# A gated S5 and attention layer: chunk outputs with C loaded once, transfers spread over three queues, and TensorE's order written out

## The chip, the core and the metric

The kernel runs on one core of a Trainium2 chip. The metric is the device time of one execution in microseconds (us). TensorE multiplies (its results go to PSUM, in banks of 128 x 512 float32), VectorE and ScalarE evict PSUM and do the elementwise work, GpSimd does elementwise work in SBUF only, and SyncE (SP) issues transfers. ScalarE and GpSimd can issue transfers as well; each engine runs its instructions, the issues among them, strictly in the order in which they stand in its program.

## The reference, cut to what matters

One layer on x (512 tokens, 1024 channels), all in float32:

```python
h = rms_norm(x, norm_w)
u_s, z_s, q, k, v, z_a, r_s, r_a = split(h @ w_in)      # 1024 -> 9216 columns
# S5 branch: 64 groups of 16 channels, 64 complex states each
#   state[t] = Abar * state[t-1] + Bbar @ u[t];   y = Re(C @ state) + D * u
g = gelu(y);  y_s = (g * sigmoid(g @ w_glu) * silu(z_s)) @ w_ssm_out
# three groups of dilated sliding-window attention, merged by their softmax sums
y_a = (attention(q, k, v) * silu(z_a)) @ w_attn_out
out = x + (sigmoid(r_s) * y_s + sigmoid(r_a) * y_a) @ w_o
```

## The kernel before, in words

**Matmuls.** Every weight matmul is done as three in a rounded format, with operands split into a high and a low part: `mm3` (lines 107 to 110). `load_w` (162) fetches a weight tile (SP issues it, line 166), ScalarE makes the high part (line 93), VectorE the low part (line 95). There are two raw slots and three split slots. A channel-major unit, `cm_unit` (172), is 8 x 3 matmuls of 128x512, accumulated in one of three PSUM banks named `pj`. In what follows such a unit with its eviction is a *filler*: za (4 of them), zs (8), rs (8), ra (8) for the gates, v0 for the values of group 0. The token-major unit v (`v_granule`, 572) has 96 matmuls of half the width. The list `order` (127 to 128) says in which order they are taken, and `plan` lists the weight loads in the same order. rs and ra end in a tanh on ScalarE (lines 469, 477) and a store to DRAM; zs ends in a product on VectorE and a store. `n_ra` ra units are in `order`, the others stand in the last attention round (lines 1018 to 1023), between scores and values and after the values.

**The S5 branch.** The sequence is cut into 64 blocks of 8 tokens, and the groups of channels into 8 *chunks* of 8 groups.
- `u_unit` (256) brings u of a chunk to DRAM, `load_u` (238) reloads it with positions on the partitions.
- *State stage*: `w_unit` (263) makes the chunk's input coefficients (VectorE, GpSimd and VectorE again: `coef`, 244 to 254) and transposes them into W; `x_unit` (275) makes from W and u the input of the scan.
- *Scan*: some 75 VectorE steps over all groups (`scan_work`, 636 to 640), traced in ten portions with a filler ahead of each.
- *Chunk outputs* (lines 755 to 787): `ca_unit` (667) loads C of the chunk, swaps its halves on GpSimd, transposes both and forms the output coefficients in one of three buffers `ab` (line 418); `m_unit` (692) forms a table M: eight small matmuls, four copies on ScalarE, the D term added on GpSimd (703), a store to DRAM (704) and a reload in another arrangement (707). `s_unit` (712) copies the states (eight copies on ScalarE), `y_unit` (724) multiplies U by M and the states by the coefficients, `g_unit` (738) transposes the result back and applies GELU into `gT_hi` and `gT_lo`. The loop over j traces m(j+2), a filler, y(j), ca(j+3), the reload of U(j+2), s(j+1), g(j-1).
- After it stands the GLU matmul (958 to 970).

**What sets the order.** The kernel is written with a framework that puts each engine's instructions in order itself: a planner simulates the program and takes, for each engine, the ready instruction that was traced first. The order of the trace is thus a priority, and where an instruction isn't ready by the planner's clock, a later one goes ahead of it. The order is fixed when the program is built. Small PSUM results share four banks (`bank`, 85). Tiles named by a `tag` share memory: a new tile waits until the last user of the old one is done.

Of the kernel before, what the change touches and what calls it, by code (L numbers as in the profile page):

```python
# [20 lines left out]
P = 128  # L21
# [4 lines left out]
G = 64  # L26
# [26 lines left out]
def tile_hybrid_block(ctx: ExitStack, tc: tile.TileContext, x, positions, norm_w, w_in, lam_re, lam_im,  # L53
                      log_dt, b_re, b_im, c_re, c_im, d_skip, w_glu, q_norm_w, k_norm_w, w_ssm_out,
                      w_attn_out, w_o, out, dbg=None):
    nc = tc.nc
    pe, act, dve, pool, sp = nc.tensor, nc.scalar, nc.vector, nc.gpsimd, nc.sync
    dbg = dbg or {}
# [53 lines left out]
    plan, loaded, look = [], [], 2  # L112
    n_ra = 2
    lo_w = [dve]
# [141 lines left out]
    def u_unit(j, ps=None):  # L256
        if ps is None:
            ps = cm_unit(hT_hi, hT_lo)
        uT = t2k("uT")
        act.copy(uT.rearrange("p (h r c) -> p r c h", h=2, r=4), ps.rearrange("p (r c h) -> p r c h", r=4, h=2))  # L260
        sp.dma_start(ud[j].rearrange("q g s c -> g q (s c)"), uT)

    def w_unit(j):
        ba = ab[j % 2][:, 0:8 * T * Q].rearrange("p (g k q) -> p g k q", g=8, k=T)
        g8 = slice(8 * j, 8 * j + 8)
        coef(ba, j, BB[:, g8], BB2[:, g8], 1, T + 1, ab[2], pool)
        W = big.tile([P, 8, P], F32, name="W", tag=("s6a", "s6b")[j % 2])
# [138 lines left out]


    dd = big.tile([P, 4, G, Q], F32, name="dd", tag="s1")
    D1, D2, BB, BB2 = (dd[:, i] for i in range(4))
# [21 lines left out]
    pool.memset(sgn[64:128], -1.0)  # L431

    Ws = {}

# [25 lines left out]
    def zs_unit(c):  # L460
        ps = cm_unit(hT_hi, hT_lo)
        z = t2k("z")
        silu2(z, ps)
        sp.dma_start(gd[0, c], z)

    def rs_unit(c):
        ps = cm_unit(hT_hi, hT_lo)
        th = t2k("th")
        act.activation(th, ps, AF.Tanh, scale=0.5)
        sp.dma_start(gd[1, c], th)  # L470
# [193 lines left out]
    pool.memset(zer, 0.0)  # L664
    sp.dma_start(kd[:, :, :, 128:240].rearrange("j q g k -> (j q) g k"), zer)

    def ca_unit(j):

        cn = sml.tile([P, 2, P], F32, name="cn")
        rows = slice(j * P, (j + 1) * P)  # L670
        sp.dma_start(cn[:, 0, 0:64], c_re[0].rearrange("g p n -> (g p) n")[rows])
        sp.dma_start(cn[:, 0, 64:128], c_im[0].rearrange("g p n -> (g p) n")[rows])
        pool.tensor_copy(cn[:, 1, 0:64], cn[:, 0, 64:128])
        pool.tensor_copy(cn[:, 1, 64:128], cn[:, 0, 0:64])
        ps = bank("cps")
        for i in range(2):
            pe.transpose(ps[:, i * P:(i + 1) * P], cn[:, i], ident)
        p12 = sml.tile([P, 2, 8, Q], F32, name="p12")
        p12f = p12.rearrange("p a g q -> p a (g q)")
        dve.tensor_scalar(p12f[:, 0], ps[:, 0:P], sgn, None, op0=ALU.mult)  # L680
        act.activation(p12f[:, 1], ps[:, P:2 * P], AF.Copy, scale=-1.0)
        ca = ab[j % 3].rearrange("p (g k q) -> p g k q", g=8, k=9)
        for h in range(2):
            coef(ca[:, 4 * h:4 * h + 4], 2 * j + h, p12[:, 0, 4 * h:4 * h + 4], p12[:, 1, 4 * h:4 * h + 4], 0, 9,
                 abt[:, 3 * nca:], dve)

        dg = sml.tile([Q, 8, Q], F32, name="dg")
        sp.dma_start(dg.rearrange("q g p -> q (g p)"), d_skip[0:1, rows].to_broadcast([Q, P]))
        pool.tensor_tensor(dg, dg, ident[0:Q, 0:Q].unsqueeze(1).broadcast_to([Q, 8, Q]), op=ALU.mult)
        return ca, dg  # L690

    def m_unit(j, ca, dg):

        kt = big.tile([Q, 8, T, Q], F32, name="kt", tag=("s7a", "s7b")[j % 2])
        ps = bank("kps")
        for gg in range(8):
            a, b = gg % 4, gg // 4
            pe.matmul(ps[32 * a:32 * a + Q, b * P:(b + 1) * P], BB[:, 8 * j + gg, :], ca[:, gg, 1:9, :],
                      start=True, stop=True, skip_group_check=True, tile_position=(0, 32 * a))
        kv = kt.rearrange("q (b a) k p -> q a b (k p)", a=4)  # L700
        for a in range(4):
            act.copy(kv[:, a], ps[32 * a:32 * a + Q, 0:2 * P].rearrange("q (b m) -> q b m", b=2))
# [4 lines left out]
        sp.dma_start(M.rearrange("p (g k) -> p g k", g=8),  # L707
                     bass.AP(tensor=kj.tensor, offset=kj.offset, ap=[[Q, T], [8 * 240, Q], [240, 8], [1, P]]))
        M = M.rearrange("p (g k) -> p g k", g=8)
        return M  # L710
# [43 lines left out]

    cas, dgs, Ms, Us, Ss_, ysbs = {}, {}, {}, {}, {}, {}
    for j in range(3):
        cas[j], dgs[j] = ca_unit(j)
        if j < 2:
            Ms[j] = m_unit(j, cas[j], dgs[j])
    n_scan = 10  # L760
    for i in range(n_scan):
        filler()
        for f in scan_work[i * len(scan_work) // n_scan:(i + 1) * len(scan_work) // n_scan]:
            f()

    uss = big.tile([P, 4, 512], F32, name="uss", tag="s6b")
    for j in range(2):
        Us[j] = load_u(j, uss[:, j % 2])
    Ss_[0] = s_unit(0)
    for j in range(8):  # L770
        if j + 2 < 8:
# [9 lines left out]
        if j > 0:  # L781
            g_unit(j - 1, ysbs.pop(j - 1))
    if fill:
        filler()
# [310 lines left out]
```

## Time and profile before

| | |
|---|---|
| median of 3 runs | 743.52 us (743.5 to 743.62) |
| profiled execution | 745.33 us, its span 743.5 us |
| mean granted TensorE clock | 0.983 |
| TensorE, VectorE, ScalarE, GpSimd busy | 94%, 63%, 45%, 23% of the span |
| moved by DMA | 85.51 MB, 115 GB/s in the mean |

A row of the profile names the line of the kernel, the engine, the operation, the output tile and its inputs, and the shapes; `x` and a number is a count. In rows of groups there follow busy time in us, the mean of one in ns, and the idle time of the engine before them with what ended it. In a timeline the first two numbers are start and duration in us. SPq is SP's queue of issues. PE is TensorE, DVE VectorE, ACT ScalarE, POOL GpSimd. A float32 matmul of the small kind stands as two records.

### The profile page before, as it was taken

To read this page: it belongs to the slowest core of one execution; us is meant where nothing else is said; L and a number is where in the kernel's file an instruction comes from. 1 tells how busy PE (TensorE), PEld (TensorE's weight loads), DVE (VectorE), ACT (ScalarE), POOL (GpSimd) and SP (SyncE) were. 2 spreads that over 40 slices of the span, in tenths; PEclk is the share of its full clock that TensorE was granted. 3 is DMA by queue.
4 is the path that set the end of the run, shared out by engine and by line. 5 is a ranking of instruction groups with operands and counts; after the bars stand their busy time and mean duration, and the time that the engine had idled before them with its cause. 6 is when DMAs were issued, how large, how long until landed. Compare 5 with 4: busy or idle time off the path is not lost.

```text
span 743.5 us, 13321 instructions
## 1 busy us (share of the span) xinstructions
PE 702.2 (94%) x5221; PEld 615.8 (83%) x5221; DVE 468.4 (63%) x958; ACT 336.7 (45%) x628; POOL 168.7 (23%) x304
## 2 busy tenths in 40 slices
PE   3699999999979688999999999999999999999998
PEld 2687788788857477888899999899999989778997
DVE  6768757989867454674336679667747654536631
ACT  6443544233388574433143475464446435433310
POOL 3345631110001001550001224142304311200000
PEclk9899999999999899999999999999999999999999
DMA  9754654674637765447324212213211321356321
GB/s 203 129 143 110 159 114 105 144 178 118 120 101 138 136 132 143 154 133 217 91 80 120 86 57 85 59 30 98 85 46 57 95 77 57 109 179 226 124 100 57
DMA packets 156014, 85.51 MB, mean 115 GB/s; under 512 B 40232, under 2 KB 148144, under 8 KB 155824
## 3 DMA queue, kind: packets, MB, share of 16 engines
q1 hardware_dynamic: 155936, 84.66, 44.1%
q8 instruction: 41, 0.67, 0.4%
q14 instruction: 21, 0.17, 0.1%
q10 hardware_dynamic: 16, 0.00, 0.0%
HBM read 73.18 MB, written 11.47 MB: 114 GB/s over the span
## 4 chain that ended last, share of the span: by engine, by line
PE 78%; DMA 8%; DVE 6%; SPq 3%; ACT 2%; issue 2%; POOL 0%; DVEq 0%; ACTq 0%
PE pj L110 21%; PE pj L109 21%; PE pj L108 21%; DMA w_raw<-in_w_in_dram 4%; PE ot L926 3%; PE ptp L940 2%; PE sps L870 2%; PE qtp L827 1%; DMA kd<-kt 1%; DVE w_lo L95 1%; PE xps L282 1%; DMA dd<-kd 1%; PE wps L271 1%; DMA gd<-th 1%; DVE scn L610 1%
## 5 line engine op out<-in xcount | busy, mean ns | idle before, releaser
L93 ACT ACTIVATE w_hi<-w_raw 128x1024 fp32r<-128x1024 f32 x100 | 105.9, 1060 | 200.6 <-PE pj L109 89.4
L95 DVE TENSOR_TENSOR w_lo<-w_raw,w_hi 128x1024 fp32r<-128x1024 f32 x98 | 124.2, 1268 | 64.1 <-ACT w_hi L93 62.9
L108 PE MATMUL pj<-hT_hi,w_hi 128*128 128x512 f32 (+1 forms) x344 | 135.0, 395 | 9.7 <-ACT w_hi L93 5.6
L109 PE MATMUL pj<-w_lo,hT_hi 128*128 128x256 f32 x512 | 144.0, 281 | 0.0
L110 PE MATMUL pj<-w_hi,hT_lo 128*128 128x256 f32 x512 | 143.9, 281 | 0.0
L108 PE MATMUL pj<-w_hi,hT_hi 128*128 128x256 f32 x512 | 143.8, 281 | 0.0
L109 PE MATMUL pj<-hT_lo,w_hi 128*128 128x512 f32 (+1 forms) x344 | 133.5, 389 | 0.4 <-DVE hT_lo L228 0.4
L110 PE MATMUL pj<-hT_hi,w_lo 128*128 128x512 f32 (+1 forms) x344 | 133.3, 388 | 0.1
L109 PEld LDWEIGHTS pj<-w_lo,hT_hi 128*128 128x128 f32 x512 | 96.2, 188 | 1.4 <-issue 0.7
L108 PEld LDWEIGHTS pj<-w_hi,hT_hi 128*128 128x128 f32 x512 | 96.0, 188 | 1.1 <-issue 0.9
L110 PEld LDWEIGHTS pj<-w_hi,hT_lo 128*128 128x128 f32 x512 | 96.0, 188 | 0.7
L108 PEld LDWEIGHTS pj<-hT_hi,w_hi 128*128 128x128 f32 x344 | 67.0, 196 | 23.1 <-ACT w_hi L93 5.8
L110 PEld LDWEIGHTS pj<-hT_hi,w_lo 128*128 128x128 f32 x344 | 66.5, 193 | 14.5 <-issue 0.8
L109 PEld LDWEIGHTS pj<-hT_lo,w_hi 128*128 128x128 f32 x344 | 66.8, 194 | 13.5 <-DVE hT_lo L228 0.8
L814 POOL TENSOR_TENSOR rt<-qraw,tC 128x256 f32<-128x256 f32 x12 | 16.5, 1371 | 127.0 <-DVE qraw L807 93.0
L109 PE MATMUL pj<-w_lo,mT_hi 128*128 128x256 f32 x128 | 36.2, 283 | 0.0
L110 PE MATMUL pj<-w_hi,mT_lo 128*128 128x256 f32 x128 | 36.2, 283 | 0.0
L108 PE MATMUL pj<-w_hi,mT_hi 128*128 128x256 f32 x128 | 36.2, 283 | 0.0
L849 ACT ACTIVATE Pt<-Pt,st 128x256 f32<-128x256 f32 (+1 forms) x64 | 31.0, 487 | 5.0 <-DVE st L847 4.8
L799 DVE TENSOR_REDUCE ssq<-qsq 128x8 f32<-128x512 f32 x24 | 16.4, 685 | 26.3 <-ACT qsq L798 26.2
L835 ACT ACTIVATE qkp<-qtp,wcol 128x512 fp32r<-128x512 f32 (+1 forms) x32 | 20.7, 685 | 20.7 <-PE qtp L827 15.6
L796 ACT COPY qraw<-pj 128x512 f32<-128x512 f32 x24 | 14.1, 586 | 35.0 <-PE pj L110 34.8
(272 smaller groups left out, 1368.5 us busy)
## 6 DMA issues: line engine op xcount, KB each, us to landing
w_raw<-in_w_in_dram SPq DMA_DIRECT2D x40, 512.0 KB
w_raw<-in_w_in_dram SPq DMA_DIRECT2D x64, 256.0 KB
dd<-kd SPq DMA_DIRECT2D x8, 512.0 KB
w_raw<-in_w_glu_dram SPq DMA_DIRECT2D x8, 512.0 KB
w_raw<-in_w_ssm_out_dram SPq DMA_DIRECT2D x8, 512.0 KB
w_raw<-in_w_o_dram SPq DMA_DIRECT2D x8, 512.0 KB
x_all<-in_x_dram SPq DMA_DIRECT2D x4, 512.0 KB
ud<-uT SPq DMA_DIRECT2D x8, 256.0 KB
```

What stands on the lines that cost most here:

```text
L93: act.activation(hi, src, AF.Copy, scale=scale)
L95: e.tensor_tensor(lo, src, hi.bitcast(F32), op=ALU.subtract)
L108: pe.matmul(o, lh, rh, start=first, stop=False, skip_group_check=True)
L109: pe.matmul(o, lh, rl, start=False, stop=False, skip_group_check=True)
L110: pe.matmul(o, ll, rh, start=False, stop=last, skip_group_check=True)
L799: dve.tensor_reduce(sq[:, 2 * b:2 * b + 2], s.rearrange("p (r h d) -> p r h d", r=2, h=4), AX.X, ALU.add)
L814: pool.tensor_tensor(t1, rh[:, :, :, 0:16], cv.broadcast_to([P, NB * 2, 2, 16]), op=ALU.mult)
L835: act.activation(hi, ps[sl], AF.Copy, scale=w)
L849: act.activation(o, o, AF.Exp, bias=nm, scale=-1.0, accum_out=st[:, kind, 1, h, b:b + 1])
L870: pe.matmul(pss[h][:, cols], QT[x_][po, 0, cb], KA[y_][po, ks], start=n == 0, stop=n == 2, skip_group_check=True)
L926: pe.matmul(o, v, pts[h][:, (2 * i + k) * P:(2 * i + k + 1) * P], start=first, stop=kind == 1 and b == NB - 1 and k == 1, skip_group_check ...
L940: pe.transpose(ps[:, (2 * i + k) * P:(2 * i + k + 1) * P], Pt[:, h, kind, 2 * bb + i, k * P:(k + 1) * P], ident)
```

## The change: what it does

- C is loaded as a whole into one tile by two transfers on ScalarE's queue; the swapped transposes are taken by two matmuls with an identity. Before, each chunk had two loads on SP's queue and two copies on GpSimd. D is loaded once and transposed; each chunk then multiplies the identity with its column.
- `ca_unit` is cut in two: `p_unit` (transposes and their two scalings, both on ScalarE now) and `ca_unit` (the coefficients). The coefficients have four buffers instead of three, and the product's temporary has a tile of its own. ca(3) is traced ahead of the loop, ca(j+4) in it.
- Queues: the reloads of u, the zs stores, the stores and reloads of the kernel tables go to GpSimd's; the stores of u, rs and ra go to ScalarE's. The weights stay on SP's.
- TensorE's order: with `issue_after`, each block of the loop is put behind the last TensorE instruction traced before it. The filler goes first in each chunk, and a filler stands ahead of the loop.
- The order of fillers: rs ahead of v0 and v, and four ra units in `order` instead of two.
- The table kt has one buffer instead of two; W's two buffers are one tile.

```diff
+    class pe:
+        @staticmethod
+        def matmul(*a, **k):
+            last[0] = nc.tensor.matmul(*a, **k)
...
+    def queued():
+
+        return tc.issue_after(last[0].ins)
...
-    n_ra = 2
+    n_ra = 4
...
-    order = [("za", c) for c in range(NP)] + [("zs", c) for c in range(KT)] + [("v0", 0), ("v", 0)]
-    order += [("rs", c) for c in range(KT)] + [("ra", c) for c in range(n_ra)]
+    order = [("za", c) for c in range(NP)] + [("zs", c) for c in range(KT)] + [("rs", c) for c in range(KT)]
+    order += [("v0", 0), ("v", 0)] + [("ra", c) for c in range(n_ra)]
...
-        sp.dma_start(Uj, ud[j].rearrange("q g s c -> s q g c"))
+        pool.dma_start(Uj, ud[j].rearrange("q g s c -> s q g c"))
...
-        sp.dma_start(ud[j].rearrange("q g s c -> g q (s c)"), uT)
+        act.dma_start(ud[j].rearrange("q g s c -> g q (s c)"), uT)
...
+    cna = big.tile([P, 8, P], F32, name="cn", tag="s6a")
+    act.dma_start(cna[:, :, 0:64], c_re[0].rearrange("(j g) p n -> (g p) j n", j=8))
+    act.dma_start(cna[:, :, 64:128], c_im[0].rearrange("(j g) p n -> (g p) j n", j=8))
...
-    abt = big.tile([P, 4096], F32, name="ab", tag="s5")
-    ab = [abt[:, i * nca:(i + 1) * nca] for i in range(3)]
+    abt = big.tile([P, 4 * nca], F32, name="ab", tag="s5")
+    ab = [abt[:, i * nca:(i + 1) * nca] for i in range(4)]
...
-        sp.dma_start(gd[0, c], z)
+        pool.dma_start(gd[0, c], z)
...
-        sp.dma_start(gd[1, c], th)
+        act.dma_start(gd[1, c], th)
...
-        sp.dma_start(rad[c], th)
+        act.dma_start(rad[c], th)
...
+    def p_unit(j):
+
         ps = bank("cps")
-        for i in range(2):
-            pe.transpose(ps[:, i * P:(i + 1) * P], cn[:, i], ident)
+        pe.transpose(ps[:, 0:P], cna[:, j], ident)
+        for h in range(2):
+            pe.matmul(ps[64 * h:64 * h + 64, P:2 * P], cna[:, j, 64 - 64 * h:128 - 64 * h], ident, start=True, stop=True,
+                      skip_group_check=True)
         p12 = sml.tile([P, 2, 8, Q], F32, name="p12")
         p12f = p12.rearrange("p a g q -> p a (g q)")
-        dve.tensor_scalar(p12f[:, 0], ps[:, 0:P], sgn, None, op0=ALU.mult)
+        act.activation(p12f[:, 0], ps[:, 0:P], AF.Copy, scale=sgn)
         act.activation(p12f[:, 1], ps[:, P:2 * P], AF.Copy, scale=-1.0)
...
-        sp.dma_start(kd[j, :, :, 0:128], kt.rearrange("q g k p -> q g (k p)"))
+        pool.dma_start(kd[j, :, :, 0:128], kt.rearrange("q g k p -> q g (k p)"))
...
-        sp.dma_start(M.rearrange("p (g k) -> p g k", g=8),
+        pool.dma_start(M.rearrange("p (g k) -> p g k", g=8),
...
     n_scan = 10
     for i in range(n_scan):
         filler()
         for f in scan_work[i * len(scan_work) // n_scan:(i + 1) * len(scan_work) // n_scan]:
             f()
-
+        if i == 1:
+            p_unit(3)
     uss = big.tile([P, 4, 512], F32, name="uss", tag="s6b")
     for j in range(2):
         Us[j] = load_u(j, uss[:, j % 2])
     Ss_[0] = s_unit(0)
+    cas[3] = ca_unit(3)
+    filler()
     for j in range(8):
+        with queued():
+            filler()
         if j + 2 < 8:
-            Ms[j + 2] = m_unit(j + 2, cas[j + 2], dgs[j + 2])
-        filler()
-        ysbs[j] = y_unit(j, cas.pop(j), Ms.pop(j), Us.pop(j), Ss_.pop(j))
-        if j + 3 < 8:
-            cas[j + 3], dgs[j + 3] = ca_unit(j + 3)
+            with queued():
+                Ms[j + 2] = m_unit(j + 2, cas[j + 2])
+        with queued():
+            ysbs[j] = y_unit(j, cas.pop(j), Ms.pop(j), Us.pop(j), Ss_.pop(j))
+        if j + 4 < 8:
+            with queued():
+                p_unit(j + 4)
+            cas[j + 4] = ca_unit(j + 4)
...
-            g_unit(j - 1, ysbs.pop(j - 1))
-    if fill:
+            with queued():
+                g_unit(j - 1, ysbs.pop(j - 1))
+    with queued():
         filler()
```

More of the change, by code (lines that the diff above doesn't have):

```diff
@@ L56, in tile_hybrid_block, with transpose @@
     nc = tc.nc
-    pe, act, dve, pool, sp = nc.tensor, nc.scalar, nc.vector, nc.gpsimd, nc.sync
+    act, dve, pool, sp = nc.scalar, nc.vector, nc.gpsimd, nc.sync
+    last = [None]
+    class pe:
+        @staticmethod
+        def matmul(*a, **k):
+            last[0] = nc.tensor.matmul(*a, **k)
+        @staticmethod
+        def transpose(*a, **k):
+            last[0] = nc.tensor.transpose(*a, **k)
+    def queued():
+        return tc.issue_after(last[0].ins)
     dbg = dbg or {}
@@ L266, in w_unit @@
         coef(ba, j, BB[:, g8], BB2[:, g8], 1, T + 1, ab[2], pool)
-        W = big.tile([P, 8, P], F32, name="W", tag=("s6a", "s6b")[j % 2])
+        W = wt[:, j % 2]
         for h in range(2):
@@ L405, in tile_hybrid_block @@
         pool.tensor_scalar(A4[sl, 0, 1], ATv[sl, 1, h, :, 0], -1.0, None, op0=ALU.mult)
+    d64 = scr([G, Q])
+    act.dma_start(d64, d_skip[0].rearrange("(g q) -> g q", g=G))
+    dcol = cst.tile([Q, G], F32, name="dcol")
+    ps = bank("dps")
+    pe.transpose(ps[0:Q, 0:G], d64, ident[:G, :G])
+    act.copy(dcol, ps[0:Q, 0:G])
+    cna = big.tile([P, 8, P], F32, name="cn", tag="s6a")
+    act.dma_start(cna[:, :, 0:64], c_re[0].rearrange("(j g) p n -> (g p) j n", j=8))
+    act.dma_start(cna[:, :, 64:128], c_im[0].rearrange("(j g) p n -> (g p) j n", j=8))
     dd = big.tile([P, 4, G, Q], F32, name="dd", tag="s1")
@@ L431, in tile_hybrid_block @@
     pool.memset(sgn[64:128], -1.0)
+    wt = big.tile([P, 2, 8, P], F32, name="W", tag="s6b")
     Ws = {}
@@ L664, in tile_hybrid_block @@
     pool.memset(zer, 0.0)
[L665 to L674, printed above, removed]
+    pool.dma_start(kd[:, :, :, 128:240].rearrange("j q g k -> (j q) g k"), zer)
@@ L687, in ca_unit, with m_unit @@
+    def m_unit(j, ca):
         dg = sml.tile([Q, 8, Q], F32, name="dg")
[L688 to L694, printed above, removed]
+        pool.tensor_tensor(dg, ident[0:Q, 0:Q].unsqueeze(1).broadcast_to([Q, 8, Q]),
+                           dcol[:, 8 * j:8 * j + 8].unsqueeze(2).broadcast_to([Q, 8, Q]), op=ALU.mult)
+        kt = big.tile([Q, 8, T, Q], F32, name="kt", tag="s7a")
@@ L753, in g_unit @@
         split(gT_hi[:, j], gT_lo[:, j], q, scale=0.5)
[L755 removed]
+    cas, Ms, Us, Ss_, ysbs = {}, {}, {}, {}, {}
     for j in range(3):
[L757 removed]
+        p_unit(j)
+        cas[j] = ca_unit(j)
         if j < 2:
[L759 removed]
+            Ms[j] = m_unit(j, cas[j])
     n_scan = 10
```

13 lines of the change are left out of this document (9 added, 4 removed).

## Prediction

> **What bounds the kernel now.** I read the page first, then busy time by stretch, then TensorE's waits, its order of instructions, and what the other engines do in the same stretch.
>
> ```profile
> span 743.5 us, 13321 instructions
> PE 702.2 (94%) x5221; PEld 615.8 (83%) x5221; DVE 468.4 (63%) x958; ACT 336.7 (45%) x628; POOL 168.7 (23%) x304
> ```
>
> TensorE is busy 702.2 of 743.5 us, so a gain can only come from the 41 us in which it is idle and from stretches in which it is slow. Busy time by stretch (first the scan, from the last state unit on, then the chunk outputs), once for all work and once for the weight-stream matmuls alone (tile pj):
>
> ```profile
> core 0: us, PE busy (x) PEld busy (x) DVE busy (x) ACT busy (x) POOL busy (x), PEclk, DMA share, GB/s
> 118.00:204.80 86.80, 86.80 (x464) 70.39 (x464) 79.22 (x110) 29.67 (x49) 12.22 (x14) 1.00 0.60 135
> 204.80:292.50 87.70, 71.48 (x798) 56.84 (x797) 49.42 (x71) 62.24 (x139) 7.61 (x19) 0.92 0.61 125
> ```
>
> ```profile
> 118.00:204.80 86.80, 84.00 (x402) 68.40 (x402) 6.12 (x9) 7.00 (x12) 1.00 0.60 135
> 204.80:292.50 87.70, 43.95 (x170) 32.88 (x169) 0.00 (x0) 5.28 (x9) 0.92 0.61 125
> ```
>
> In the scan TensorE never rests and VectorE is busy 79.2 of 86.8 us. In the chunk outputs TensorE is idle 16.2 us and its clock falls to 0.92. Only 170 wide matmuls stand there, 7 fillers of 24 (rs3 to rs7, ra0, ra1): the planner ran TensorE ahead during the scan and used up the rest. What TensorE waits for there, and its order in time:
>
> ```profile
> PE kps L698 <- DVE ab L254: 5.8, 2, 3.4
> PE pj L108 <- ACT th L469: 4.1, 1, 4.1
> PE yps L731 <- issue: 2.6, 1, 2.6
> PE yps L733 <- ACT uss L721: 2.1, 1, 2.1
> PE yps L731 <- DMA dd<-kd: 1.5, 1, 1.5
> ```
>
> ```profile
> 222.67 0.41 PE L698 MATMUL kps<-ab,dd 128*16 128x128 f32 x8
> ...
> 226.15 0.48 PE L108 MATMUL pj<-hT_hi,w_hi 128*128 128x512 f32 x1
> 226.47 0.40 PE L109 MATMUL pj<-hT_lo,w_hi 128*128 128x512 f32 x1
> ...
> 231.60 0.40 PE L110 MATMUL pj<-hT_hi,w_lo 128*128 128x512 f32 x1
> ...
> 245.50 0.79 PE L108 MATMUL pj<-hT_hi,w_hi 128*128 128x512 f32 x1 [4.10 <-ACT th L469]
> 246.09 0.63 PE L109 MATMUL pj<-hT_lo,w_hi 128*128 128x512 f32 x1
> 246.52 0.63 PE L110 MATMUL pj<-hT_hi,w_lo 128*128 128x512 f32 x1
> ```
>
> From 226.47 to 231.60 lie 22 matmuls, 0.233 us each: a filler is 24 of them, 5.6 us. One chunk's own work (m, y, p, g units) takes 222.67 to 226.15, 3.5 us. So 170 x 0.233 + 8 x 3.5 = 67.7 us at most fill 87.7 us: **at least 20 us are lost** in this stage, 16.2 as idle time and the rest because after a wait of 4.1 us the matmuls start 0.43 us apart. These 20 us are what the change can win.
>
> **The change, part by part.** *TensorE's order.* Every block of a chunk now stands behind the block before it, so TensorE cannot run past y(0), which needs the end of the scan. Ahead of y(0) stand za3, zs0-7, rs0-2. Before, v0 and v were done there too: 24 wide matmuls (5.6 us) and 96 of half width. Thirteen fillers are 312 wide ones, 72.8 us, and 84.0 - 72.8 leaves 11.2 us for the 96. TensorE thus reaches y(0) 16.8 us sooner, and after m(2) (0.7 us, from two pieces like the one at 222.67) stands there at 204.8 - 16.8 + 0.7 = 188.7. Queued behind it are p(4) and rs3, and behind those the stores and evictions that read them.
>
> *When y(0) may start.* That is VectorE's scan:
>
> ```profile
> 117.54 0.35 DVE L680 TENSOR_SCALAR p<-cps,sgn 128x128 f32<-128x128 f32 x1 [4.76 <-PE cps L677]
> ...
> 204.89 0.69 DVE L612 TENSOR_TENSOR Xs<-Xs,scn 128x512 f32<-128x512 f32 x1
> ```
>
> ```profile
> L95 DVE TENSOR_TENSOR w_lo<-w_raw,w_hi 128x1024 fp32r<-128x1024 f32 x14 | 17.3, 1239 | 5.7 <-ACT w_hi L93 5.6
> ...
> L253 DVE TENSOR_TENSOR ab<-p,AT 128x576 f32<-128x576 f32 x7 | 5.2, 749 | 0.0
> ```
>
> ```profile
> 207.33 0.34 PE L733 MATMUL yps<-ab,uss 128*64 128x64 f32 x4 [2.10 <-ACT uss L721]
> ```
>
> The scan ends at 204.89 + 0.69 = 205.6 and y(0)'s state half starts 1.75 us later. Three weight splits fewer: -3.7. The 5.7 us that VectorE stands before a split, because the weights land late on SP's crowded queue: -3.5 of them. Three p scalings (0.35) go to ScalarE: -1.0. ca(0) no longer waits for its C transpose, so its six operations of 0.75 fit partly into the 4.76 us of idle time at 117.5: -2.5 of 4.5. ca(3) has a buffer of its own and slips into the scan, five operations more than today: +3.7. Sum -7.0: scan end 198.6, y(0) at 200.3. With every wait won back and ca(3) left behind the scan it is 192, with no wait won back and nothing brought forward 208. I take 200.3, the middle of the two. TensorE idles about 11.6 us before y(0), and starts slow again: 12 matmuls at 0.43 instead of 0.233 is 2.3 us, of which I count 2.0.
>
> *From y(0) to the first GLU matmul.* Left are rs3-7, v0, v (worth two), ra0-3: 12 fillers' worth, 67.2 us, and 8 x 3.5 = 28: 95.2 us. ScalarE must keep up. In the second stretch it is busy 62.24 us over 139 instructions, 0.448 each, and a full chunk has 20 of them (state copies 8, kt 4, g 4, y, th, w_hi, p 1 each): 9.0 us. It gains the second p scaling and the issue of a store:
>
> ```profile
> L681 ACT ACTIVATE p<-cps 128x128 f32<-128x128 f32 x4 | 1.1, 280 | 0.1
> ```
>
> ```profile
> 237.39 1.44 SPq L470 DMA_DIRECT2D gd<-th  x1
> 238.92 0.38 SPq L166 DMA_DIRECT2D w_raw<-in_w_in_dram  x1
> ...
> 247.75 1.86 SPq L470 DMA_DIRECT2D gd<-th  x1
> ```
>
> An issue holds its queue 0.38 to 1.86 us; on ScalarE's, every eviction of PSUM stands behind it. With 0.38 a chunk needs 9.7 us against TensorE's 9.1, 0.6 over in the four full chunks, 2.4 us; the later chunks lack m and p units, which takes about as much off the 95.2. At 1.86 in six chunks it would be 9 us more; six issues of 0.38 are nearest to an unblocked queue, which the removal of 16 C and 8 d_skip transfers makes likelier. So 95 us.
>
> *Two gates moved.* GLU starts at 200.3 + 95 + 2.0 = 297.3, against 292.5 + 11.2 = 303.7 for the same work (two fillers come from the end): **-6.4 us**. Their old place must not need them. There, after the last score block:
>
> ```profile
> 651.75 1.69 PE L940 MATMUL ptp<-ident,Pt 128*128 128x128 f32 x14
> ```
>
> ```profile
> L903 DVE TENSOR_SCALAR Pt<-Pt,sd x8: 274/340/343, 638.9 to 640.6; 128x256 f32<-128x256 f32 x6, 128x128 f32<-128x128 f32 x2
> L903 DVE TENSOR_SCALAR Pt<-Pt,sfb x8: 335/341/354, 640.9 to 644.4; 128x256 f32<-128x256 f32 x8
> ```
>
> The first transposes start at 651.75 although their tiles are scaled at 640.6 and the last at 644.4: 7 to 11 us of cover are spare, and two fillers are 11.2. I cost it at nothing; with the cover gone it is 11.2 - 7.4 = 3.8 us.
>
> *GpSimd's queue.* It takes the reloads of U (16 in all), the kernel tables' stores and loads, the zs stores. No GpSimd DMA stands in this trace. Per chunk two of them move 128 rows in eight pieces each. Where this bites is the state stage, in whose chain GpSimd multiplies:
>
> ```profile
> L253 POOL TENSOR_TENSOR ab<-dd,AT 128x1024 f32<-128x1024 f32 x8 | 21.2, 2655 | 16.6 <-DVE ab L254 14.2 <-DVE dd L427 2.4
> ```
>
> Between its eight multiplications GpSimd has 14.2 us of waiting for VectorE, 1.8 each; an issue below that is hidden, one above delays the scan by the difference, eight times. From below 0.38 (SP's row), from above GpSimd's own longest step, 2.7: nothing to 7 us. I take 1 us. Early loads of C (the same bytes, sooner) and 20 stores' issue on ScalarE: -1 to +3, I take 0.7. The Trainium skill, "DMA: Bandwidth & Descriptors", section "Latency and other measured facts", gives about 1 us to the first byte from GpSimd, 0.6 from SP. As an estimate by that page alone, the 1 us would be 0 and the sum 1 us better; no run here shows it.
>
> A wait is added: GpSimd's load of table M waits for its own store's landing, and the next U reload, the d_skip product and the zeroing of the next state tile stand behind it. Its length now:
>
> ```profile
> 253.86 1.49 ACT L702 COPY kt<-kps 16x256 f32<-16x256 f32 x4 [3.43 <-PE kps L698]
> ```
>
> ```profile
> 255.91 2.65 DMA kd<-kt
> 258.58 8.20 DMA dd<-kd
> ```
>
> From kt's copies to M's landing 258.58 + 8.20 - 253.86 = 12.9 us; two chunks are 2 x 9.7 = 19.4. It fits, with 6 us to spare.
>
> **Sum:** -6.4 + 1.0 + 0.7 = -4.7 us. The profiled execution took 745.33 us (1.8 beside its span), so it becomes 740.6; the median of the runs shown is 743.52, which becomes **738.8 us**.
>
> **Rivals.** *Short stall.* The scan ends at its early bound, y(0) at 192, and the queues cost nothing: 8.3 + 1.7 more, 728.8. For it: 5.7 us of VectorE's waits are for late weights. Against it: the planner fills bubbles of the scan with ca(3), as it did with one operation of it.
>
> *The landings stay.* The reason for the 4.1 us wait was a gate's store:
>
> ```profile
> 237.39 6.86 DMA gd<-th
> ```
>
> Its landing, not its place in the queue, is the longer part. If landings stay 7 to 8 us, the 3.5 us of VectorE's waits are not won and the 1.5 us for table M (last row of TensorE's waits) come back: 738.8 + 5.0 = 743.8, no change. The Trainium skill, "DMA: Bandwidth & Descriptors", section "Issuing engines are not separate DMA queues", speaks for it: all issuing engines share 16 DMA engines, and several issuers save issue time only. The row agrees so far: the issue itself took 1.44 us, the landing 6.86. Against it: in order, SP stands before a store that isn't ready and holds the weights behind.
>
> *GpSimd becomes the chain (slower).* Each issue of a U reload holds GpSimd 3 us or more. Then the state stage grows by 8 x (3 - 1.8) = 9.6 us where I count 1, TensorE has no filler left to cover it, and the time is 738.8 + 8.6 = 747.4; it decides the sign from 1.8 + 5.7/8 = 2.5 us. At 3.5 us it is 751. Against it: SP issues the like in under 2 us.
>
> *The order isn't what changes.* If TensorE ran that order anyway, nothing would stall before y(0); but v0 and v stand ahead of it in the trace, so the order does change. I give it nothing of its own.
>
> **How the numbers follow.** Forecast 0.42 (its own range 735 to 743), short stall 0.16, landings stay 0.17, GpSimd 0.20, 0.05 for anything else. The range 729 to 752 takes in all four. About 0.2% (1.5 us) is what a measurement of this kernel tells from no change. Faster: 0.37 of the forecast, the short stall, 0.06 of the third: 0.59. Same: 0.05 + 0.07 + 0.01 = 0.13. Slower: 0.04 + 0.20 + 0.04 = 0.28.
>
> **What would show it.** Right: one wait of TensorE of 9 to 14 us before the first yps on uss, the scan's last step near 198, then twelve fillers with waits under 3 us in all and GLU near 297. The chunk stage ScalarE-bound: its waits small, TensorE's on kt or ysb. Wrong: TensorE waits for M or U inside the chunks, GpSimd's issues above 2 us, the state stage ending well after 118, or the transposes at the end waiting for scaled tiles.

## The result and the profile after

The changed kernel takes **770.25 us** (median of four runs, 767.51 to 772.19) against 743.51 for the kernel before in the same comparison: a ratio of 1.036 (95% interval 1.032 to 1.040). It is slower; I had forecast 738.8 with a range up to 752. The profiled execution took 767.51 us, the fastest of the four, so the rows below account for the 22.2 us by which the profiled span grew and not for the whole 26.7 us between the medians.

The rows on span and engines on the page of the changed kernel:

```profile
span 765.7 us, 13338 instructions
PE 703.3 (92%) x5246; PEld 616.4 (81%) x5246; DVE 459.3 (60%) x950; ACT 340.3 (44%) x637; POOL 201.1 (26%) x329
```

TensorE is busy as long as before (703.3 against 702.2 us), so nearly all of the loss is idle time. Its waits from 217 us, just ahead of y(0), to the GLU (total, times, longest):

```profile
PE yps L63 <- ACT uss L751: 20.3, 1, 20.3
PE yps L63 <- DMA dd<-kd: 5.9, 2, 5.3
PE yps L63 <- ACT th L498: 1.6, 1, 1.6
PE vtp L67 <- ACT vt L592: 1.4, 1, 1.4
```

Nearly all of the loss lies ahead of the GLU matmul. The rows of its first matmuls, with the start of the first and the last of them, before and after:

```profile
L108 PE MATMUL pj<-gT_hi,w_hi x64: 389/389/398, 292.5 to 335.4; 128*128 128x512 f32 x64
```

```profile
L63 PE MATMUL pj<-gT_hi,w_hi x52: 389/389/398, 325.2 to 359.9; 128*128 128x512 f32 x52
```

It starts at 325.2 instead of 292.5. Of these 32.7 us, 11.2 are the two gates moved there; 21.5 are lost, and the span grew by 22.2. Busy time by stretch, from the scan to y(0) and from there to the GLU (columns as in the prediction):

```profile
118.00:218.09 100.09, 78.97 (x493) 61.23 (x488) 81.68 (x113) 36.00 (x67) 18.34 (x25) 0.92 0.52 125
218.09:325.20 107.11, 98.31 (x981) 82.07 (x981) 49.30 (x67) 68.64 (x146) 23.80 (x31) 0.95 0.54 118
```

TensorE's timeline at y(0):

```profile
196.87 0.63 PE L63 MATMUL kps<-ab,dd 128*16 128x128 f32 x16
197.43 0.34 PE L63 MATMUL yps<-dd,uss 128*64 128x64 f32 x4
218.09 0.48 PE L63 MATMUL yps<-ab,uss 128*64 128x64 f32 x4 [20.33 <-ACT uss L751]
218.34 0.45 PE L63 MATMUL yps<-dd,uss 128*64 128x64 f32 x4
```

TensorE reaches y(0) at 197.4, stands for 20.33 us, and starts again slowly. What it waits for is VectorE's scan. VectorE's groups inside the scan, from 129.5 to 215.5:

```profile
L110 DVE TENSOR_TENSOR w_lo<-w_raw,w_hi 128x1024 fp32r<-128x1024 f32 x12 | 14.6, 1220 | 3.2 <-ACT w_hi L108 3.1
L639 DVE TENSOR_TENSOR scn<-Xs,scn 128x1024 f32<-128x1024 f32 x8 | 9.9, 1235 | 10.2 <-ACT Xs L300 10.0
L269 DVE TENSOR_TENSOR ab<-ab,cat 128x576 f32<-128x576 f32 x8 | 6.3, 782 | 0.0
L268 DVE TENSOR_TENSOR cat<-p,AT 128x576 f32<-128x576 f32 x8 | 6.0, 749 | 0.0
L267 DVE TENSOR_TENSOR ab<-p,AT 128x576 f32<-128x576 f32 x8 | 5.7, 747 | 1.1 <-ACT p L707 1.1
```

Two things are to be seen. Before its first step VectorE stands 10.0 us for the scan's input: the scan starts at 129.5, where it started at 119.3. And all four ca lie inside it, 24 operations of 18.0 us, where there were 18 of 13.3. This row shows, for the kernel before, the scan's steps that read its input, with the start of the first and of the last:

```profile
L610 DVE TENSOR_TENSOR scn<-Xs,scn x8: 1215/1220/1226, 119.3 to 202.9; 128x1024 f32<-128x1024 f32 x8
```

The start is late because the state stage is. GpSimd's timeline there:

```profile
80.28 3.99 POOL L268 TENSOR_TENSOR ab<-dd,AT 128x1024 f32<-128x1024 f32 x1 [2.85 <-DVE ab L269]
84.22 1.39 POOL L256 DMA_DIRECT2D Uj<-ud  x1
85.63 2.84 POOL L268 TENSOR_TENSOR ab<-dd,AT 128x1024 f32<-128x1024 f32 x1
88.41 2.62 POOL L256 DMA_DIRECT2D Uj<-ud  x2
```

And the first reload in the timeline of SP's queue in the kernel before:

```profile
74.79 0.62 SPq L241 DMA_DIRECT2D Uj<-ud  x1
```

The issue of a reload takes GpSimd 1.3 to 1.4 us, no more; but the first reload stands behind a multiplication that waits for VectorE, and so is issued at 84.22 instead of 74.79. (4.3 us of that is the multiplication's own delay, which began at 75.99 before.) Inside the chunks, ScalarE's copies of one kernel table start at 250.21; then GpSimd's timeline:

```profile
250.21 1.48 ACT L732 COPY kt<-kps 16x256 f32<-16x256 f32 x4
```

```profile
251.77 1.26 POOL L733 TENSOR_TENSOR kt<-kt,dg 16x128 f32<-16x128 f32 x1 [1.40 <-ACT kt L732]
252.98 1.30 POOL L256 DMA_DIRECT2D uss<-ud  x1
254.28 0.13 POOL L744 MEMSET uss<- 128x8 f32 x1
254.32 0.56 POOL L734 DMA_DIRECT2D kd<-kt  x1
...
262.74 1.33 POOL L737 DMA_DIRECT2D dd<-kd  x1 [7.46 <-DMA kd<-kt]
```

The first matmul that reads this table, in TensorE's timeline:

```profile
273.07 0.48 PE L63 MATMUL yps<-dd,uss 128*64 128x64 f32 x4 [5.33 <-DMA dd<-kd]
```

The store of kt needs about 8 us to land, the U reload stands in front of it, and TensorE can read table M at 273.07: 22.9 us after the copies began. ScalarE's copies of the next tables wait for this landing too (3.1 us in two waits), as kt has one buffer now; what that costs was not tried.

### The profile page after: what moved, and what is told of

Read it like the earlier page. It is cut to its first block, busy times and chain, and to the rows that moved or that the text cites. A ratio compares the mean times of both kernels' runs of the same rounds, so it can differ in the third digit from the quotient of the medians.

```text
span 765.7 us, 13338 instructions
## 1 busy us (share of the span) xinstructions
PE 703.3 (92%) x5246; PEld 616.4 (81%) x5246; DVE 459.3 (60%) x950; ACT 340.3 (44%) x637; POOL 201.1 (26%) x329
## 4 chain that ended last, share of the span: by engine, by line
PE 74%; DMA 9%; DVE 4%; issue 4%; SPq 3%; POOL 3%; ACT 1%; DVEq 0%; POOLq 0%; ACTq 0%
PE pj L63 62%; DMA kd<-kt 3%; PE sps L63 3%; PE ot L63 2%; DMA w_raw<-in_w_in_dram 2%; DMA Uj<-ud 2%; PE ptp L67 2%; DMA dd<-kd 2%; PE qtp L67 1%; PE yps L63 1%; POOL ab L268 1%; DVE scn L639 1%; PE xps L63 1%; DVE w_lo L110 1%; SPq L208 1%
## 5 line engine op out<-in xcount | busy, mean ns | idle before, releaser
L108 ACT ACTIVATE w_hi<-w_raw 128x1024 fp32r<-128x1024 f32 x100 | 105.9, 1060 | 206.9 <-PE pj L63 171.9
L110 DVE TENSOR_TENSOR w_lo<-w_raw,w_hi 128x1024 fp32r<-128x1024 f32 x98 | 119.9, 1225 | 72.6 <-ACT w_hi L108 71.8
L63 PE MATMUL yps<-ab,uss 128*64 128x64 f32 x256 | 18.5, 245 | 20.3 <-ACT uss L751 20.3
L63 PEld LDWEIGHTS yps<-ab,uss 128*64 128x64 f32 x256 | 15.8, 160 | 20.4 <-issue 20.4
```

Of the source, the lines that this page charges most:

```text
L63: last[0] = nc.tensor.matmul(*a, **k)
L108: act.activation(hi, src, AF.Copy, scale=scale)
L110: e.tensor_tensor(lo, src, hi.bitcast(F32), op=ALU.subtract)
```

## The experiments

Each line of the table is one kernel; all times are us. *Scan* is VectorE's first step to the end of its last, *y(0)* the first state matmul with TensorE's wait before it, *chunks* the stretch from there to the first GLU matmul. These come from one profiled execution each, which lies up to 2.7 us from the median; *time* is the median, the ratio is to the kernel before beside it, with its 95% interval.

| kernel | scan | y(0), wait | chunks | time | ratio |
|---|---|---|---|---|---|
| before | 119.3 to 205.6 | 207.3, 2.1 | 85.2 | 743.5 | |
| after | 129.5 to 215.4 | 218.1, 20.3 | 107.1 | 770.3 | 1.036 (1.032 to 1.040) |
| e1 order free | 131.1 to 222.2 | 224.7, 6.1 | 88.2 | 755.9 | 1.015 (1.012 to 1.018) |
| e2 U on SP | 122.4 to 208.3 | 211.0, 17.6 | 106.5 | 760.3 | 1.021 (1.020 to 1.023) |
| e3 C late | 128.7 to 214.6 | 217.3, 20.3 | 110.6 | 767.7 | 1.031 (1.027 to 1.035) |
| e4 before + order | 118.9 to 200.0 | 202.6, 13.4 | 94.0 | 750.0 | 1.007 (1.005 to 1.010) |
| e5 e2 + M on SP | 121.7 to 211.8 | 214.5, 21.7 | 107.8 | 766.2 | 1.031 (1.028 to 1.035) |
| e6 e2 + order free | 121.2 to 211.4 | 215.1, 3.6 | 91.6 | 749.5 | 1.007 (1.005 to 1.010) |
| e7 e5 + order free | 120.7 to 214.2 | 217.8, 6.8 | 89.2 | 750.0 | 1.008 (1.005 to 1.010) |
| e8 before + splits on GpSimd | 118.9 to 204.7 | 209.0, 2.6 | 87.6 | 747.0 | 1.003 (1.000 to 1.005) |
| e9 e2 + ca(3) behind | 124.5 to 207.2 | 210.0, 14.4 | 107.3 | 758.8 | 1.020 (1.016 to 1.024) |
| e10 before + ca(2) behind | 119.2 to 197.3 | 204.3, 0 | 89.0 | 745.7 | 1.002 (1.000 to 1.003) |
| e11 before + queues but U | 119.7 to 207.6 | 209.3, 3.6 | 86.7 | 746.1 | 1.003 (1.002 to 1.005) |
| e12 e10 and e11 | 118.8 to 196.9 | 203.9, 0 | 91.3 | 748.0 | 1.006 (1.004 to 1.008) |
| e13 e2 and e3 | 118.2 to 204.2 | 206.9, 17.6 | 107.4 | 759.3 | 1.020 (1.016 to 1.025) |
| e14 e2 + M early | 120.2 to 206.2 | 208.9, 17.6 | 104.5 | 757.7 | 1.018 (1.015 to 1.022) |
| e15 e2 + v ahead | 120.9 to 208.3 | 211.0, 12.9 | 103.9 | 758.2 | 1.019 (1.016 to 1.021) |
| e16 e9, e13, e14, e15 | 119.9 to 205.1 | 207.8, 10.8 | 99.1 | 750.5 | 1.008 (1.005 to 1.011) |
| e17 e16 + two fillers ahead | 120.0 to 203.8 | 216.4, 0 | 89.6 | 748.8 | 1.007 (1.004 to 1.010) |
| e18 e16 + order free | 118.0 to 202.0 | 205.7, 4.1 | 95.5 | 746.2 | 1.003 (1.001 to 1.005) |

**The order: e1, e4, and the pairs.** e1 frees the order in the changed kernel; e4 writes it into the kernel before, with nothing else of the change.

```diff
 def queued():
-    return tc.issue_after(last[0].ins)
+    return nullcontext()          # e1
```

> The changed kernel, but TensorE's order is left to the planner again (no block is put behind the block before it). Theory A, the written order is what costs: TensorE's one wait of 20.3 us before y(0) is filled with fillers that now stand behind it, GLU starts some 15 us sooner, and the time falls from 770 to 752 to 756. Theory B, the late scan and the chunks' transfers cost: fillers used up ahead of y(0) are missing in the chunks, TensorE waits there instead (as it did before the change, 16 us), and the time stays at 764 to 771.

> The kernel before, with TensorE's order written out as in the change and nothing else of it (old queues, old buffers, old order of fillers, the filler first in each chunk). Theory A, the order by itself costs: TensorE stands 15 to 20 us before y(0), which cannot move because the scan ends at 205 as before; the ten fillers and the chunks' own work left behind it take 84 us or more, so GLU starts at 300 to 305 instead of 292.5 and the time is 751 to 757. Theory B, the order is harmless and only the queues cost: what is lost before y(0) is won back in the chunks, 742 to 746.

e1: 755.9, as theory A had it; the stall falls from 20.3 to 6.1 us. e4: 750.0, 1 us better than A's range, since the scan ended 5.6 us sooner there, with 12 splits in it instead of 14. The first row of TensorE's waits in e4:

```profile
PE yps L63 <- ACT uss L736: 13.4, 1, 13.4
```

Five pairs, each with and without the written order: a stall of 10.8 us goes with a loss of 4.3 (e16 and e18), 13.4 with 5.6 (e4 and before), 17.6 with 10.9 (e2 and e6), 20.3 with 14.3 (after and e1), 21.7 with 16.2 (e5 and e7). (The kernel before differs by up to 0.8 us between the two comparisons of a pair; the times of the first pair overlap.) So **all but 5 to 8 us of the stall is lost**. But the kernels with a free order stand there too, for 2.1 to 6.8 us: the written order adds 6.7, 11.3, 14.0, 14.2 and 14.9 us of stall and costs 4.3, 5.6, 10.9, 14.3 and 16.2. What the fillers saved for the chunks give back is thus 5.7 us at most (e4) and nothing at the two longest stalls, not the 16 that I had counted on (18.0 us lost in the chunks before, 1.8 in my 97).

**The queues: e2, e3, e5, e6, e7, e13.**

```diff
-        pool.dma_start(Uj, ud[j]...)
+        sp.dma_start(Uj, ud[j]...)              # e2, e5 to e7, e9, e13 to e18
-    act.dma_start(cna...)
+    with tc.issue_after(u_last[0].ins):     # behind uT(2): e3, e13, e16 to e18
+        act.dma_start(cna...)
-        pool.dma_start(kd[j]...); pool.dma_start(M...)
+        sp.dma_start(kd[j]...); sp.dma_start(M...)   # e5, e7
```

> The changed kernel, but the reloads of U are issued on SP's queue again. Theory B: the first Uj is issued some 9 us sooner, TensorE's four waits for Uj (5.8 us) go, the scan starts near 123 instead of 129.5, y(0) follows it, and the time falls by 6 us to 764. Theory A: the scan's start moves little since the coefficients' chain on VectorE and GpSimd sets it, the time stays within 2 us of 770. Rival: SP's queue, full of weights, delivers U late in the chunks and the time grows above 772.

> The changed kernel, but the two loads of C are issued on ScalarE's queue only behind uT(2), some 50 us later. Theory B: the third weight comes 3 to 4 us sooner (its high part near 30 instead of 33.9), everything up to the scan moves by as much, and the time falls by 4 us to 766. Theory A or a chain that does not go through the weights: the scan starts at 129.5 as before and the time is 769 to 771. Rival: the moved loads now delay U's stores and reloads, time above 772.

> The changed kernel with U's reloads on SP's queue (760.3 alone) and the loads of C behind uT(2) (767.7 alone). If the early loads of C are what is left of the late start, hidden so far behind U's reloads, the scan starts at 119 instead of 122.4 and the time is 756 to 758. If something else delays it (p on ScalarE, the tiles), the start stays near 122 and the time within 1.5 us of 760.

U back on SP's queue brings 9.9 us, more than the 6 expected, and the scan starts 7.1 us sooner. C loaded later brings the third weight's high part back to 29.7 us (33.9 after), but the scan starts only 0.8 us sooner and the time moves by 2.6, with ranges that overlap (764.7 to 770.2 against 767.5 to 772.2). With U out of the way the same edit moves the scan's start by 4.1 us, to 1.1 us ahead of where it was before. The scan's first step in VectorE's timeline of e13:

```profile
118.24 1.23 DVE L641 TENSOR_TENSOR scn<-Xs,scn 128x1024 f32<-128x1024 f32 x1 [5.51 <-ACT Xs L301]
```

So of the late start, U on GpSimd's queue accounts for some 7 us and the early C loads for some 4 (together a little more than the 10.2), hidden behind U as long as it is there. In the time e13 is 1.0 us below e2, inside its own spread (757.0 to 763.6); what the 4.1 us are worth there stays open.

> The changed kernel with the reloads of U, and also the stores and reloads of the kernel tables (kd, M), on SP's queue again; TensorE's written order stays. Compared with the run in which only U went back (760.3). Theory C, the round trip of M on GpSimd's queue costs inside the chunks: TensorE's wait for dd<-kd of 3.4 us goes and the time falls to 755 to 757. Theory A, with the written order all that counts is when the scan ends: within 1.5 us of 760. Rival: kd's store waits on SP in front of the weights, and the time grows above 762.

> The changed kernel with two parts undone together: TensorE's order left to the planner, and U's reloads on SP's queue. If the two losses are separate, they add: 770 less 14.3 (order alone) less 9.9 (U alone) is 746. If the fillers cover the late scan once the order is free, an earlier scan is worth little more: 752 to 756, as with the order alone.

> As the run before it, with the stores and reloads of the kernel tables on SP's queue as well: of the change there are left C loaded once, p on ScalarE, four coefficient buffers, the stores on ScalarE's queue and the order of the fillers. Theory, the two moved queues and the order are the whole loss: 742 to 745, as before the change or a little better. Rival, the scan still holds all 24 coefficient operations (18.0 us of VectorE, against 13.3 for 18 before): 747 to 750.

e5 falsifies theory C: with the tables back on SP the time grows by 5.9 us, to 766.2. VectorE's weight splits in the scan of e2, by groups:

```profile
L110 DVE TENSOR_TENSOR w_lo<-w_raw,w_hi 128x1024 fp32r<-128x1024 f32 x12 | 14.7, 1224 | 2.5 <-ACT w_hi L108 2.3
```

The same group in e5:

```profile
L110 DVE TENSOR_TENSOR w_lo<-w_raw,w_hi 128x1024 fp32r<-128x1024 f32 x12 | 14.8, 1235 | 6.8 <-ACT w_hi L108 6.8
```

And two rows of the waits of SP's queue in the scan of e5:

```profile
SPq L734 <- POOL dg L722: 7.8, 1, 7.8
SPq L737 <- DMA kd<-kt: 6.9, 3, 3.1
```

A store that isn't ready holds the weights behind it on SP, and VectorE stands 4.3 us longer. The Trainium skill, "DMA: Bandwidth & Descriptors", section "Issuing engines are not separate DMA queues", says that several issuers save the issue time only. The trace disagrees in both directions: the choice of the issuer, and with it what a transfer stands behind and holds up in that engine's program, was worth 9.9 us for U (1.3 to 1.4 us an issue on GpSimd, 0.8 in the median on SP in the state stage of e2) and 5.9 us for M (0.6 us an issue on SP in the scan of e5). e6 (749.5) lies 3.5 us above the sum of the two separate gains (746): most of them add. e7 (750.0, spread 746.1 to 751.9) cannot be told from e6 and is the rival's number: with the order and the queues of U and the tables undone, the change is still slower than the kernel before.

**The coefficients in the scan, and what the scan is worth: e9, e10, e8.**

```diff
-    cas[3] = ca_unit(3)
+    with tc.issue_after(scan_end[0].ins):
+        cas[3] = ca_unit(3)       # e9, e16 to e18; e10: ca_unit(2) in the kernel before
```

> The changed kernel with U's reloads on SP's queue (760.3 by itself), and the coefficients ca(3) put behind the last step of the scan on VectorE. Theory D, the coefficients brought into the scan delay y(0): six operations of 0.75 us leave the scan, it ends 4.5 us sooner, and since TensorE's written order cannot use the stall, all of it is won: 756. Rival, M(3) then comes too late for its chunk or the chunks' own waits set the end: 759 to 762.

> The kernel before with one edit: the coefficients ca(2) are formed behind the last step of the scan instead of inside it. Theory D holds for the old order too: VectorE's scan is 4.5 us shorter, two or three fillers fewer run ahead of y(0) and stand in the chunks: 739 to 741. Rival: table M(2) is late for y(2), TensorE waits there for what it gained: 743 to 747.

In e9 the scan takes 82.7 us instead of 85.9, but starts later in this kernel; the time, 758.8 (755.7 to 760.7), is not told from 760.3 and lies between the theory's 756 and the rival's 759. e10 is the plainest run of the study: the scan ends 8.3 us sooner, y(0) comes only 3.0 us sooner and **nothing is won** (745.7). Its stretches:

```profile
118.00:204.28 86.28, 86.28 (x456) 69.88 (x456) 77.89 (x108) 32.40 (x56) 7.60 (x10) 1.00 0.52 127
204.28:293.30 89.02, 71.91 (x810) 56.37 (x809) 51.07 (x73) 59.41 (x132) 10.27 (x23) 0.92 0.60 132
```

And TensorE's waits in the second of them:

```profile
PE pj L108 <- ACT th L469: 8.9, 4, 4.5
PE kps L700 <- DVE ab L254: 3.7, 1, 3.7
PE yps L733 <- issue: 3.0, 1, 3.0
```

TensorE, in the planner's order, works off fillers until 204.3, and the chunks take 3.8 us longer, with 8.9 us of waits for the tanh of the gates and 3.7 for the coefficients that left the scan. e8 takes ten splits off VectorE:

```diff
+    lo_w[0] = pool      # ahead of the scan; back to dve behind it
```

> The kernel before with one edit of another kind: the low parts of the ten weights fetched in the scan are formed on GpSimd instead of VectorE. Theory, VectorE's scan sets when y(0) may start, and this is what should have been relieved: ten splits of 1.24 us leave VectorE, the scan ends 9 to 12 us sooner, fillers are saved for the chunks, and the time is 732 to 737. Rival: GpSimd's 2.7 us or more for each split makes weights late, or slows VectorE's own steps, and the time is 742 to 748.

The scan becomes only 0.5 us shorter. Two of VectorE's groups from 118 to 205 us, 1.27 and 0.75 us each before:

```profile
L610 DVE TENSOR_TENSOR scn<-scn 128x1024 f32<-128x1024 f32 x6 | 12.4, 2066 | 0.0
L254 DVE TENSOR_TENSOR ab<-ab 128x576 f32<-128x576 f32 x6 | 9.1, 1524 | 0.0
```

One such step in VectorE's timeline:

```profile
140.85 3.71 DVE L610 TENSOR_TENSOR scn<-scn 128x1024 f32<-128x1024 f32 x1
```

And GpSimd's timeline from 132 us to the same moment:

```profile
132.87 6.69 POOL L95 TENSOR_TENSOR w_lo<-w_raw,w_hi 128x1024 fp32r<-128x1024 f32 x1
...
141.10 2.38 POOL L95 TENSOR_TENSOR w_lo<-w_raw,w_hi 128x1024 fp32r<-128x1024 f32 x1
```

The step, 1.21 us at its shortest in this run, takes 3.71 when a split of GpSimd runs in it (1.21 and 2.38 make 3.59), and a split among VectorE's steps took 6.69 instead of 2.38. The time, 747.0, is the rival's.

**What the rest of the change is worth: e11, e12.** Both are the kernel before, with the change's queues for everything but U and C (e11), and with ca(2) behind the scan besides (e12).

```diff
-        sp.dma_start(kd[j]...); sp.dma_start(M...); sp.dma_start(gd[0, c], z)
+        pool.dma_start(kd[j]...); pool.dma_start(M...); pool.dma_start(gd[0, c], z)
-        sp.dma_start(gd[1, c], th); sp.dma_start(rad[c], th)
+        act.dma_start(gd[1, c], th); act.dma_start(rad[c], th)
```

> The kernel before with the change's queues but for U: kernel tables and zs stores on GpSimd's, rs and ra stores on ScalarE's; U and C stay on SP's, TensorE's order is the planner's. Theory, the queue moves other than U's do what I predicted of them: the waits for weights in the scan (5.7 us) fall by 3 to 4 us, TensorE's wait for a tanh whose store held the queue (4.1 us) goes: 738 to 741. Rival, M's longer landing on GpSimd's queue or the stores on ScalarE give it back: 743 to 747.

> The two edits of the runs before it together: ca(2) behind the scan, and the change's queues but for U, in the kernel before. If both shorten the scan, they add to about 735 (733 to 738). If only one of them works, 739 to 742; if the chunks' transfers become the bound, 743 or more.

746.1 and 748.0: both are the rivals' numbers. In the kernel before the other queue moves bring nothing either, though in e11 the wait of 4.1 us for a tanh in the chunks falls to 1.3. In its place TensorE stands 10.3 us (two waits, one of 8.0) ahead of multiplications by a table M; the profile names no releaser for them. And VectorE's waits for weights in the scan, which should have fallen from 5.7 us by 3 to 4, rise:

```profile
L95 DVE TENSOR_TENSOR w_lo<-w_raw,w_hi 128x1024 fp32r<-128x1024 f32 x14 | 17.2, 1226 | 7.9 <-ACT w_hi L93 7.7
```

**The chunk stage and the fillers: e14 to e18.**

```diff
-            Ms[j + 2] = m_unit(j + 2, ...)      # ahead of y(j)
+            Ms[j + 3] = m_unit(j + 3, ...)      # e14, e16 to e18: directly behind y(j)
-    order = ... + rs + [v0, v] + ra
+    order = ... + [v0, v] + rs + ra             # e15 to e18
-    filler()
+    for _ in range(3): filler()                 # e17, ahead of the chunks
```

> The changed kernel with U's reloads on SP's queue, and m(j+3) directly behind y(j) instead of m(j+2) behind the next filler: each table M sets out one filler (5.6 us) sooner. If M's round trip lengthens the chunk stage, TensorE's wait for dd<-kd (3.4 us) and the slow clock behind it go, the stage shrinks from 106.5 to 100 to 102 us and the time is 755 to 757. If it is the stores' landing behind the tanh tiles or the own work of a chunk, the stage stays at 105 to 107 and the time at 759 to 762.

> The changed kernel with U's reloads on SP's queue and the old order of fillers: v0 and v (16.8 us) stand ahead of y(0), rs behind it; TensorE's order is still written out. If the written order costs only by its stall, the wait of 17.6 us before y(0) shrinks to 4 us or less (three more splits delay the scan by up to 3.7), and the time is 747 to 751, as with the order left free (749.5). If pinning the blocks costs by itself, it stays above 755.

> The changed kernel with four edits: U on SP's queue, C loaded later, tables M one filler earlier, v0 and v ahead of y(0), and ca(3) behind the scan. If what was found adds up: scan from 119 to about 203, no stall above 4 us, a chunk stage near 85 us for nine fillers, GLU at 291 to 296, and the time is 735 to 740, below the kernel before. If the chunk stage keeps its 10 us of waits whatever stands ahead of it, 743 to 748.

> The kernel of the four edits (750.5, stall before y(0) 10.8 us) with two more fillers traced ahead of the chunks: 11.2 us of matmuls fill the stall, two more splits (2.4 us) lengthen the scan. If the stall is the whole cost of the written order, it shrinks to 2 to 4 us and the time is 742 to 745. If each filler taken away from the chunks comes back there as waits, the stage shrinks by less than 11 us, and the time stays at 748 to 752.

> The kernel of the four edits with TensorE's order left to the planner. By the earlier pairs (a stall of 13.4, 17.6, 20.3 and 21.7 us cost 5.6, 10.9, 14.3 and 16.2 us, so the first 6 to 8 us of a stall cost nothing) a stall of 10.8 us is worth 3 to 5 us: 745 to 748. If the planner's order uses the fillers up as in the kernel before and the early tables M then cover the chunks: 741 to 744, better than before.

e14: the waits for M go, but 4.3 us of waiting for coefficients (kps on ab) take their place; the chunks shrink by 2.0 us, the time by 2.6, between the two cases. e15: I had the edit's size wrong. Twelve units stand ahead of y(0) either way, v counts as two, so it is one filler (5.6 us) more, not 16.8; the stall fell by 4.7 and the time by 2.2, so its 758.2 does not settle whether pinning costs by itself. e16, all of it together, comes to 750.5, above both of its ranges; e18 with the order free comes to 746.2, as the pairs had it. e17 was to show whether the stall is all that the written order costs; it is not. Its two stretches:

```profile
118.00:216.37 98.37, 93.06 (x510) 74.12 (x507) 82.57 (x113) 34.93 (x63) 12.01 (x18) 0.97 0.46 120
216.37:306.00 89.63, 80.14 (x860) 63.77 (x859) 47.52 (x64) 65.30 (x141) 19.09 (x29) 0.96 0.68 137
```

The stall of 10.8 us is gone, but y(0) comes 8.5 us later than in e16 (TensorE stands 5.3 us ahead of it in two waits for a tanh of the gates) and the chunks are 9.5 shorter: the GLU starts 0.9 us sooner. No kernel here beats the one before. With the order free and U back on SP's queue, e6 is 5.1 us above the kernel before in its comparison and e18 1.9; which of e18's other edits brings the difference was not tried one by one in the free order.

## Why the prediction was wrong, point by point

The GLU was forecast for 297.3 and came at 325.2, 27.9 us later: 10.2 by the scan's start, 6.6 by its length, 1.0 between its end and y(0), 10.1 in the chunks. (For the late start the forecast had 1.7 us, added behind the 297.3.)

- **GpSimd's queue, +1.0 us: the step that failed first.** The issue itself stayed within the bounds: 1.3 to 1.4 us, under the 1.8 of cover, so nothing by the prediction's own rule, and far from the 2.5 that the rival needed. (The upper bound of 2.7 was the mean of GpSimd's multiplications, not the longest.) But I weighed only what the issue does to GpSimd, not what GpSimd does to the issue: in program order a reload stands behind a multiplication that waits for VectorE. The scan starts 7.1 us sooner when the reloads go back to SP's queue, and e2 puts their move at 9.9 us of the time. The rival "GpSimd becomes the chain" named the right place, but by a mechanism whose price the trace denies.
- **Early loads of C, in the 0.7 us**, a term for which the prediction showed no row: hidden behind U, 0.8 us of scan start by themselves, 4.1 once U is back (e3, e13).
- **The scan, -7.0 us: measured -0.4.** By the groups, the splits gave -2.7 (forecast -3.7), the waits for weights -2.5 (-3.5), the p scalings -0.3 (-1.0: a wait for ScalarE's p of 1.1 us took their place), the coefficients +4.7 (+1.2 for ca(0) and ca(3) together). The last was the failed one: ca(0) never reached the idle time ahead of the scan. In e2 VectorE stands there 5.49 us, and p(0), now on ScalarE, comes only behind the last copies of the scan's input. ScalarE's timeline in e2:

```profile
120.32 2.00 ACT L300 COPY Xs<-xps 128x256 f32<-128x256 f32 x4 [0.88 <-PE xps L63]
122.11 0.36 ACT L707 ACTIVATE p<-cps,sgn 128x128 f32<-128x128 f32 x1
```

And the scan's first step in VectorE's:

```profile
122.35 1.23 DVE L639 TENSOR_TENSOR scn<-Xs,scn 128x1024 f32<-128x1024 f32 x1 [5.49 <-ACT Xs L300]
```

  That p(0) back on VectorE would bring ca(0) forward is read from these rows and was not tried. (The prediction's late bound for y(0), 208, does not come out of its terms, which give 206.4; the 200.3 is their sum and does not rest on it.)
- **TensorE at y(0)** was forecast for 188.7; it came at 197.4, 8.7 later, because the whole front was late. That the written order makes it stand there was right; the stall was 20.3 us, not 11.6.
- **The chunks, 97 us: measured 107.1.** TensorE's busy time there is 98.3, close to my 97; the 8.9 us of waits are the miss (the four rows above without the stall). The M round trip of 12.9 us was mis-sized: counted in the same way, from the copies, it takes 22.9, with the U reload ahead and a landing of 8, and so no longer fits the 19.4 of two chunks.
- **"These 20 us are what the change can win"**, the premise, did not hold, and this was the dearest step: the written order that should win them costs 14.3 us by e1 (5.6 by itself, e4). Chunk time less 5.6 us a filler and 28 for the chunks' own work leaves 18.0 us before, 11.9 after, 10.0 in e4, 9.3 in e14, 9.5 in e16: never under 9. By the count of fillers in it, the stage took 85.2 to 91.3 us with seven (before, e10 to e12), 88.2 to 91.6 with nine (e1, e6, e7, e17), 94.0 and 95.5 with ten (e4, e18), 99.1 and 103.9 with eleven (e16, e15), 104.5 to 110.6 with twelve (the others with the written order). As far as kernels that differ in more can be compared, two fillers more than before cost at most 6.4 us of their 11.2 there, and every further one about its own 5.6. In e10 a scan ending 8.3 us sooner brought nothing. What keeps these 9 us in every order is not settled by the runs; the waits change their names (tanh, M, ab) from kernel to kernel.
- **Right in part:** the weights behind SP's stores. With the tables' stores on SP's queue VectorE waits 4.3 us longer (e5 against e2; I had 3.5), but in the kernel before the same stores taken off that queue did not shorten the waits (7.9 us in e11 for 5.7), and e4, with all stores on it, has 4.0.
- **Right:** the gates moved from the end. From the GLU to the end the kernel takes 440.5 us instead of 451.0: 10.5 of the 11.2 us came off there.

## What to carry to other kernels

A written order on the busiest engine turns each lateness of what it waits for into idle time, so fix it only where the thing waited for is surely early: here all but 5 to 8 us of the stall was lost. When a transfer changes its queue, cost what it will stand behind in that engine's program, not only what its issue costs the engine. And before counting idle time as winnable, shorten the suspected bound by itself (e10 comes nearest to that) and see whether the end moves.

## What the runs showed of the hardware that I had not expected

- VectorE and GpSimd hold each other up: the rows of e8 above, 1.21 against 3.71 us and 2.38 against 6.69. The Trainium skill, "SBUF — State Buffer", section "SBUF: two separate sides", calls the port pair that the two share an exclusive lock, held for the whole instruction, also against a VectorE operation with two SBUF inputs; the trace agrees with that.
- Stores of one kind and size took very different times within one stage. Two transfers on the chain of waits of the changed kernel:

```profile
232.15 2.75 DMA kd<-kt
...
254.32 8.13 DMA kd<-kt
```

  Which of the other transfers in flight lengthened the second was not tried.
